# A two-layer transformer kernel: the first layer's feed-forward goes over to seven block products, with its hidden values passed through DRAM

## The chip, the core and the metric

The kernel runs on one core of one Trainium2 chip. The metric is the device time of one execution in microseconds; the time of before is the median of three runs. The profile is of one more execution of the same program.

## The reference, cut to what matters

Two layers work on 1024 latent tokens and 256 context tokens of width 1024 (the context leaves after layer 0). Each layer is a mixer (attention with a second branch) and a feed-forward (SwiGLU, hidden width 2816), each followed by a residual sum and a layer norm. Six vectors per layer, the modulation, are computed from `c` and `c_ctx`.

```python
def swiglu(h, w_in, w_out):
    a, g = jnp.split(h @ w_in, 2, axis=-1)
    return (jax.nn.silu(g) * a) @ w_out

        x = layer_norm(ALPHA * x + g1 * y, ln1_g[l], ln1_b[l])
        x = layer_norm(ALPHA * x + g2 * swiglu(x * (1.0 + sc2) + sh2, ffn_w_in[l], ffn_w_out[l]), ln2_g[l], ln2_b[l])
        if with_ctx_out:
            xc = layer_norm(ALPHA * xc + cg1 * yc, ln1_g[l], ln1_b[l])
            xc = layer_norm(ALPHA * xc + cg2 * swiglu(xc * (1.0 + csc2) + csh2, ffn_w_in[l], ffn_w_out[l]),
                            ln2_g[l], ln2_b[l])
```

## The kernel before, in words

All is fp32. A matrix product is made of three fp32r matmuls: each operand is split into a high part (a cast, mostly on ScalarE) and a low part (a subtraction, on GpSimd or VectorE), and high x high, high x low and low x high are summed in PSUM (`mm3`, L234; `split`, L222). Activations stay transposed: `X[c][b]` holds channel chunk c (8 of 128 channels) of token block b, split. Blocks 0 and 1 are 512 latents each, block 2 is the 256 context tokens. A weight unit is 128 x 1024 floats: `wunit` (L227) loads it into one of two `raw` buffers, and splits it into one of three `w` buffers of the same ring.

All loads and stores are issued by SyncE (SP), in order. A scheduler that simulates the engines puts the instructions of each engine in order when the program is built; program order is the priority, and `high_priority` shifts it. The hardware keeps that order on each engine. The exception is layer 1's attention, whose order is written out by hand.

**Output projection, then feed-forward of layer 0.** `out_proj` (L974) goes over the blocks 0, 1, 2: eight output chunks of matmuls, added into `ACC` (the residual, L362), then `ln_block` (L364): transposes, statistics, normalisation in place, transposes back, and for each chunk the modulated value split into X and the residual for the next sum back into ACC. The norm of one block runs beside the matmuls of the next; that of block 2 has `early` (L559) beside it, the matmuls of hidden chunk 0 for token block 0.

`ffn` (L573) goes over the 22 hidden chunks in pairs. `hidden` (L589) makes, per chunk and block, 24 matmuls for the a half and 24 for the gate half, then `gate` (L548): silu on ScalarE, product on VectorE, split by VectorE and GpSimd into a `hid` buffer. The output weights of the pair follow, and `outs` (L607): for each block and each of eight output chunks six matmuls, then one addition into ACC on VectorE (L362). The last pair's `outs` alternate with the norm. Between these pieces `pump` takes one step at a time of the modulation of layer 1 (`ada_vec`, L306): a 512 KB load, four or eight multiply-adds on VectorE (L323, L325), and after every second step column sums on TensorE (L330). 48 such steps lie in this stage.

**Feed-forward of layer 1.** `ffn_fast` (L763) has two passes. The first makes the hidden values: chunks 0 and 1 in the usual way (`plain`, L736), the others in pairs, with seven block products in place of eight. The 8 channel chunks and the two token blocks make a 2 x 2 block matrix of the activations, and the pair of hidden chunks with the two channel halves one of the weights. `x_sums` (L696) forms sums of the activation blocks in ACC, and `t_split` (L709) splits them into T. `weights` (L785) loads the two units, splits them into two `w` tiles, makes four sums in place and splits these into two `ws` tiles, of which there are three. `blocks` (L830) makes seven products of 12 matmuls each and combines them with additions on ScalarE and VectorE. The hidden values go to DRAM (`hs`). The residual was stored to `accs` by the norm (`full`, L409). The second pass loads hidden values back into the slots of X (`hid`, L902), splits them, and does the output matmuls as above; ACC is loaded again by `load_acc`. In the last pair of the first pass, both halves do products 1, 2 and 3 first (`begin`), as products 2 and 3 free the slots of X that the second pass fills first.

```python
            for j, x in ((2, b22), (3, b12), (4, b21)):
                self.t_split(j, c, x, 'gvg'[j - 2])
...
            pair(NHC - 2, (1, 2, 3))
```

Of the kernel before, what the change touches and what calls it, by code (L numbers as in the profile page):

```python
# [17 lines left out]
P = 128  # L18
# [16 lines left out]
NV = 5  # L35
# [4 lines left out]
EARLY = ((0, 0),), ((0, 0), (0, 1))  # L40
# [14 lines left out]
FAST, LASTB = (1,), 6  # L55
# [121 lines left out]
class K:  # L177
# [128 lines left out]
    def ada_vec(self, l, v, nvec, srcs, pspool, pstag, bufs=2, q0=0, abufs=None):  # L306
# [29 lines left out]
        for q in range(q0, 4):  # L336
            for kh in range(2):
                self.side.append(lambda q=q, kh=kh: piece(q, kh))


    def acc_open(self, l, blks, first=True):
        if l in FAST and first:
# [4 lines left out]
        self.ehp, self.eh = p, {}  # L347
        self.ACC = [p.tile([P, 8, BLKN[b]], F32, name=f"ACC{l}_{b}") for b in blks]
# [15 lines left out]
    def ln_block(self, b, pools, sc=None, sh=None, acc='keep', out=None, lnb=None, eng=None, tiles=None, group=1,  # L364
# [38 lines left out]
        for c in range(8):  # L403
# [5 lines left out]
            if full:  # L409
                self.affine('a', t, pb, self.lna[:, 0, c:c + 1], self.lna[:, 1, c:c + 1])  # L410
                self.dma(self.accs[c, :, BLK0[b]:BLK0[b] + n], t)
                t = A[:, c, :]
                self.affine('av'[b == 0 or c % 2], t, pb, sc[:, c:c + 1], sh[:, c:c + 1])
                self.split(t, x[:, 0, :], x[:, 1, :], 'a', 'g' if b == 0 else 'vg'[c % 2])
                continue
# [132 lines left out]
    def gate(self, wp, tag, pa, pg, h, n):  # L548

        nc = self.nc  # L550
        sg = self.tile(wp, [P, 512], F32, tag, bufs=1 if tag == "sgx" else 2)
        nc.scalar.activation(sg[:, :n], pg[:, :n], AF.Silu)
        nc.vector.tensor_tensor(out=sg[:, :n], in0=pa[:, :n], in1=sg[:, :n], op=ALU.mult)
        self.split(sg[:, :n], h[:, 0, :n], h[:, 1, :n], 'v', 'g')

    def hidden_w(self, l, hc):
        return [self.wunit(self.I[f'fi{l}'][j * NHC + hc], 'a', 'v' if hc < 2 else 'g') for j in range(2)]

    def early(self, l, pp, wp):  # L559

        for hc, b in EARLY[l]:
            if hc not in self.eh:
                self.eh[hc] = (self.hidden_w(l, hc), {})
            (wa, wg), hb = self.eh[hc]
            pa = self.tile(pp, [P, 512], F32, "op")
            self.fm_block(pa, wa, self.X, b)
            pg = self.tile(pp, [P, 512], F32, "op")
            self.fm_block(pg, wg, self.X, b)
            hb[b] = self.tile(self.ehp, [P, 2, BLKN[b]], F32R, f"eh{hc}_{b}")
            with self.tc.high_priority(HPE) if HPE else ExitStack():  # L570
                self.gate(wp, "sgx", pa, pg, hb[b], BLKN[b])

    def ffn(self, l, blks):  # L573
        nc, tc, I = self.nc, self.tc, self.I
        gv = lambda b: self.mod[:, l, 5, 1 if b == 2 else 0, :]

        with tc.tile_pool(name=f"ffn{l}", bufs=1, reuse_waits="tile") as fp:
            side, wst = ExitStack(), ExitStack()
            wx = None
            if l == 1:  # L580
                self.ctxstack.close()
                wx = wst.enter_context(tc.tile_pool(name="wx", bufs=1, side="right", reuse_waits="tile"))
            pp = side.enter_context(tc.tile_pool(name=f"ffps{l}", bufs=8, space=PSUM, reuse_waits="tile"))
            if l == 0:
                self.adp = side.enter_context(tc.tile_pool(name="ffad", bufs=1, reuse_waits="tile"))
                for v in range(6):
                    self.ada_vec(1, v, 2 if v < 2 else 1, [I['ad1'][v * 8 + j] for j in range(8)], pp, "f", abufs=1)

            def hidden(hc):  # L589

                (wa, wg), hs = self.eh.pop(hc) if hc in self.eh else (self.hidden_w(l, hc), {})
                rest = [b for b in blks if b not in hs]
                h = self.tile(fp, [P, 2, NTOK], F32R, "hid", bufs=3)
                pas = []
                for b in rest:
                    pa = self.tile(pp, [P, 512], F32, "f")
                    self.fm_block(pa[:, :BLKN[b]], wa, self.X, b)
                    pas.append(pa)
                for b, pa in zip(rest, pas):
                    pg = self.tile(pp, [P, 512], F32, "f")  # L600
                    self.fm_block(pg[:, :BLKN[b]], wg, self.X, b)
                    hs[b] = h[:, :, BLK0[b]:BLK0[b] + BLKN[b]]
                    self.gate(fp, "sg", pa, pg, hs[b], BLKN[b])
                    self.pump(1)
                return hs

            def outs(pp, tag, hs, us, b, o=0, n=None):  # L607
                n = n or BLKN[b]
                for f in range(8):
                    ps = self.tile(pp, [P, 512], F32, tag)  # L610
                    for i, u in enumerate(us):
                        w = u.rearrange("p s (f m) -> p s f m", m=P)
                        self.mm3(ps[:, :n], w[:, 0, f], w[:, 1, f], hs[i][b][:, 0, o:o + n], hs[i][b][:, 1, o:o + n],
                                 i == 0, i == len(us) - 1)
                    self.add_out(ps, f, b, gv(b), o, n)


            end = NHC - 2
            for h0 in range(0, end, 2):
                hcs = range(h0, min(h0 + 2, end))  # L620
                hs = [hidden(hc) for hc in hcs]
                us = [self.wunit(I[f'fo{l}'][hc], 'a', 'g') for hc in hcs]
                for b in blks:
                    outs(pp, "f", hs, us, b)
            last = range(end, NHC)
            ws, us, hs = {}, {}, {hc: {} for hc in last}
            if l == 0:
                hs = {hc: hidden(hc) for hc in last}
                us = {hc: self.wunit(I['fo0'][hc], 'a', 'v') for hc in last}
            self.pump(1000)  # L630
            side.close()
            with ExitStack() as es:
                pp, pools = self.tail_pools(es, f"ft{l}", *TP[l])
                self.ltb = LTB[2]
                if l == 0:
                    vec = self.ln_vecs(0, 2, 3, 2, 1, 0, 1, "02")
                else:
                    bc = self.tile(pools[0], [P, 2, D], F32, "lnbc")
                    self.dma(bc, I['lnbc'])

                    def final(r, nt):
                        bv = bc.rearrange("p k (c m) -> p k c m", m=P)
                        n = NV if r < NLAT - 2 * P else NVL
                        for k, op in ((0, ALU.mult), (1, ALU.add)):
                            self.tt('v', nt[:, :n], nt[:, :n], bv[:, k, :n], op)
                            self.tt('g', nt[:, n:], nt[:, n:], bv[:, k, n:], op)
                        o = self.O['out'][r:r + P, :].rearrange("t (c m) -> t c m", m=P)
                        for c in (slice(0, n), slice(n, 8)) if r >= NLAT - DSP * P else (slice(0, 8),):
                            self.dma(o[:, c], nt[:, c])
                ht = {hc: self.tile(fp, [P, 2, NTOK], F32R, "hid", bufs=3) for hc in last if l}  # L650

                def last_hidden(b, o, n):
                    for hc in last:
                        if hc not in ws:
                            ws[hc] = [self.wunit(I[f'fi{l}'][j * NHC + hc], 'a', 'g', wx if hc == end else None) for j in range(2)]
                        pq = []
                        for w in ws[hc]:
                            pq.append(self.tile(pp, [P, 512], F32, "op"))
                            self.fm_block(pq[-1][:, :n], w, self.X, b, o, n)
                        t = BLK0[b] + o  # L660
                        hs[hc][b] = ht[hc][:, :, BLK0[b]:BLK0[b] + BLKN[b]]
                        self.gate(fp, "sg", *pq, ht[hc][:, :, t:t + n], n)
                    for hc in last:
# [8 lines left out]
                for k, (b, o, n) in enumerate(segs):  # L672
                    if l == 1:
                        for seg in segs[k and k + SEGA:k + SEGA + 1]:
                            last_hidden(*seg)
# [946 lines left out]
```

## Time and profile before

| | us |
|---|---|
| median of 3 runs (3249.15 to 3252.54) | 3250.75 |
| the profiled execution's own time | 3247.87 |
| its span, first to last instruction | 3246.1 |
| output projection of layer 0, about | 710 to 865 |
| feed-forward of layer 0, to the last hidden chunk | 865 to 1751 |
| first pass of layer 1's feed-forward, about | 2555 to 2983 |
| second pass, to the end | 2989 to 3246 |

The rows of a profile name the line of the kernel, the engine, the operation and out <- in by the tiles' names, with shapes, the count, busy time and mean duration. Busy times of matmuls overlap, since they are pipelined. Idle time before an instruction is put down to what ended it. Tables of windows give the busy time of each engine in a stretch, the granted clock of TensorE (1.00 is 2.4 GHz, 0.50 is 1.2 GHz), the busy share of the DMA engines and the bytes moved.

### The profile page before, as it was taken

To read this page: it belongs to the slowest core of one execution; us is meant where nothing else is said; L and a number is where in the kernel's file an instruction comes from. 1 tells how busy PE (TensorE), PEld (TensorE's weight loads), DVE (VectorE), ACT (ScalarE), POOL (GpSimd) and SP (SyncE) were. 2 spreads that over 40 slices of the span, in tenths; PEclk is the share of its full clock that TensorE was granted. 3 is DMA by queue.
4 is the path that set the end of the run, shared out by engine and by line. 5 is a ranking of instruction groups with operands and counts; after the bars stand their busy time and mean duration, and the time that the engine had idled before them with its cause. 6 is when DMAs were issued, how large, how long until landed. Compare 5 with 4: busy or idle time off the path is not lost. (4 is left out here: it accounts for less than half of the span.)

```text
span 3246.1 us, 47796 instructions
## 1 busy us (share of the span) xinstructions
PE 3140.1 (97%) x18580; PEld 2770.4 (85%) x18580; DVE 1952.3 (60%) x3385; ACT 1096.8 (34%) x1930; POOL 1421.9 (44%) x1292
## 2 busy tenths in 40 slices
PE   8899999999999999999999999999999899999998
PEld 8888999988888888888888898988888788887877
DVE  6998777766755444444224597368874544445655
ACT  2235676652311011111111434367763422222221
POOL 3665777771322222222221244247763444443344
PEclk8899999999999999999999999999999999999999
DMA  5354122132222222221111234323213122225332
GB/s 218 111 192 126 30 49 53 29 110 85 74 72 72 75 73 77 73 79 65 40 36 38 91 122 129 109 67 93 80 48 130 53 84 78 84 85 169 104 111 59
DMA packets 157010, 282.07 MB, mean 87 GB/s; under 512 B 27120, under 2 KB 97520, under 8 KB 156656
## 3 DMA queue, kind: packets, MB, share of 16 engines
q1 hardware_dynamic: 156784, 279.01, 26.9%
q8 instruction: 147, 2.41, 0.3%
q14 instruction: 79, 0.65, 0.1%
HBM read 223.64 MB, written 55.31 MB: 86 GB/s over the span
## 5 line engine op out<-in xcount | busy, mean ns | idle before, releaser
L214 POOL TENSOR_TENSOR w<-raw,w 128x1024 fp32r<-128x1024 f32 x120 | 266.4, 2225 | 629.5 <-ACT w L206 533.9
L236 PE MATMUL f<-X,w 128*128 128x512 f32 (+1 forms) x1336 | 488.3, 365 | 16.8 <-ACT w L206 7.4
L237 PE MATMUL f<-X,w 128*128 128x512 f32 (+1 forms) x1336 | 485.0, 363 | 1.6 <-POOL X L214 1.6
L238 PE MATMUL f<-X,w 128*128 128x512 f32 (+1 forms) x1336 | 479.3, 362 | 0.0
L206 ACT CAST w<-raw 128x1024 fp32r<-128x1024 f32 (+1 forms) x170 | 168.2, 998 | 796.5 <-issue 395.1
L362 DVE SCALAR_TENSOR_TENSOR ACC<-f,mod,ACC 128x512 f32<-128x512 f32 (+1 forms) x368 | 244.6, 689 | 128.0 <-PE f L238 127.5
L236 PEld LDWEIGHTS f<-X,w 128*128 128x128 f32 x1336 | 253.7, 190 | 56.9 <-DVE ACC L362 8.2
L526 PE MATMUL acc<-w,X 128*128 128x256 f32 x1008 | 293.6, 292 | 8.3 <-ACT u L1096 4.9
L325 DVE SCALAR_TENSOR_TENSOR ada<-adraw,silu_c,ada 128x256 f32<-128x256 f32 x490 | 291.2, 631 | 5.9 <-DMA adraw<-in_ad 2.9
L528 PE MATMUL acc<-w,X 128*128 128x256 f32 x1008 | 292.9, 291 | 0.0
L527 PE MATMUL acc<-w,X 128*128 128x256 f32 x1008 | 292.6, 290 | 0.0
L237 PEld LDWEIGHTS f<-X,w 128*128 128x128 f32 x1336 | 253.7, 190 | 40.4 <-POOL X L214 2.1
L238 PEld LDWEIGHTS f<-X,w 128*128 128x128 f32 x1336 | 253.1, 189 | 39.9 <-POOL w L214 0.4
L214 POOL TENSOR_TENSOR pp<-e,pp 128x512 fp32r<-128x512 f32 x156 | 203.4, 1310 | 36.2 <-ACT pp L206 30.4
L526 PEld LDWEIGHTS acc<-w,X 128*128 128x128 f32 x1008 | 199.0, 198 | 9.2 <-ACT u L1096 5.1
L527 PEld LDWEIGHTS acc<-w,X 128*128 128x128 f32 x1008 | 199.0, 197 | 0.0
L528 PEld LDWEIGHTS acc<-w,X 128*128 128x128 f32 x1008 | 199.0, 198 | 0.0
L1252 ACT ACTIVATE e<-ss 128x512 f32<-128x512 f32 x252 | 145.3, 596 | 86.1 <-PE ss L1250 79.0
L214 POOL TENSOR_TENSOR hid<-sg,hid 128x512 fp32r<-128x512 f32 (+1 forms) x65 | 77.1, 1187 | 213.2 <-DVE hid L208 201.9
L237 PE MATMUL f<-hid,w 128*128 128x512 f32 (+1 forms) x472 | 166.8, 353 | 0.0
L236 PE MATMUL f<-hid,w 128*128 128x512 f32 (+1 forms) x472 | 166.7, 353 | 0.0
L238 PE MATMUL f<-hid,w 128*128 128x512 f32 (+1 forms) x472 | 166.7, 353 | 0.0
(344 smaller groups left out, 8103.5 us busy)
## 6 DMA issues: line engine op xcount, KB each, us to landing
raw<-in_fi SPq DMA_DIRECT2D x88, 512.0 KB, 3.6
adraw<-in_ad SPq DMA_DIRECT2D x86, 512.0 KB, 3.6
raw<-in_fo SPq DMA_DIRECT2D x44, 512.0 KB, 3.5
qs<-stg SPq DMA_DIRECT2D x27, 512.0 KB, 3.9
qd<-qs SPq DMA_DIRECT2D x192, 64.0 KB, 2.3
q<-qs SPq DMA_DIRECT2D x180, 64.0 KB, 2.3
raw<-hs SPq DMA_DIRECT2D x22, 512.0 KB, 3.5
ks<-stg SPq DMA_DIRECT2D x20, 512.0 KB, 2.8
```

The lines of the kernel that those rows point to most:

```text
L206: nc.scalar.copy(out=out, in_=in_)
L214: eng.tensor_tensor(out=out, in0=a, in1=b, op=op)
L236: mm(ps, lhsT=wh, rhs=xh, start=start, stop=False)
L237: mm(ps, lhsT=wh, rhs=xl, start=False, stop=False)
L238: mm(ps, lhsT=wl, rhs=xh, start=False, stop=stop)
L325: nc.vector.scalar_tensor_tensor(out=a, in0=rv[:, k], scalar=s, in1=a, op0=ALU.mult, op1=ALU.add)
L362: self.nc.vector.scalar_tensor_tensor(out=a, in0=ps[:, :n], scalar=g[:, f:f + 1], in1=a, op0=ALU.mult, op1=ALU.add)
L526: mm(o, lhsT=xh, rhs=w[:, 0, k], start=st, stop=False)
L527: mm(o, lhsT=xh, rhs=w[:, 1, k], start=False, stop=False)
L528: mm(o, lhsT=xl, rhs=w[:, 0, k], start=False, stop=sp)
L1252: nc.scalar.activation(e, S, AF.Exp)
```

## The change

Layer 0 calls `ffn_fast` as well, and `ffn`, `hidden`, `gate`, `early` are gone. What it does:

- `out_proj` calls `early_fast` and `x_sums` for both layers; for layer 0 `early_fast` issues no matmuls, and `x_sums` makes the sums without splitting them. The norm is `full` for both layers: it stores the residual to a new DRAM tensor `accr` and leaves the modulated value in ACC. The context's ACC is a pool of its own, closed after the projection.
- Layer 0 makes chunks 0 and 1 plainly for all three blocks, then splits T, then goes over the ten pairs with seven products for the latents; the context's 256 tokens are multiplied plainly with the two `w` tiles (`ctx`).
- `weights` makes its four tiles at once, with `ws` in two buffers, and the products use them in another order (`lhs`). For both layers the last half-pair does products 1, 2, 3 (and the context) first; `begin` is gone, so the gate half of the last pair keeps the usual order. In layer 1 the a half of chunk 1 is split into a `ws` tile.
- Layer 1's modulation is pumped in both passes: vectors 0 to 2 in the first, 3 to 5 in the second, one piece after each block.
- `load_acc(0)` is issued with a priority shift of 400 in both layers.

```diff
-EARLY = ((0, 0),), ((0, 0), (0, 1))
-FAST, LASTB = (1,), 6
+LASTB, HPA = (2, 6), 400
...
+    def x_sums(self, split):
+        a, b = self.ACC[:2]
+        for c in range(4):
+            b11, b12, b21, b22 = a[:, c, :], b[:, c, :], a[:, c + 4, :], b[:, c + 4, :]
+            self.tt('v', b11, b12, b11, ALU.subtract)
+            self.tt('v', b12, b22, b12, ALU.subtract)
+            self.tt('v', b22, b22, b11, ALU.subtract)
+            self.tt('v', b21, b21, b22, ALU.subtract)
+            if split:
+                for j in (2, 3, 4):
+                    self.t_split(j, c, 'gvg'[j - 2])
...
+    def early_fast(self, l, pp):
+        self.hs = self.dram.tile([NHC, P, NTOK], F32, name=f"hs{l}")
+        self.wu, self.sg = {}, {}
+        for j, i in () if l == 0 else ((1, 0), (0, 0), (1, 1)):
+            self.plain(l, pp, "op", (j, i, 0))
+
+    def ffn_fast(self, l, blks):
...
+        if l == 0:
+            self.t_open(0)
+            for i in range(2):
+                for b in ((0, 1, 2), (1, 0, 2))[i]:
+                    for j in (1, 0):
+                        self.plain(l, pp, "f", (j, i, b))
+            for j in (2, 3, 4):
+                for c in range(4):
+                    self.t_split(j, c, 'vg'[c % 2])
+        else:
+            self.wsp = self.ws_open()
+            for x in (((1, 0, 1), (0, 0, 1), (1, 1, 1)), ((0, 1, 1),), ((0, 1, 0),)):
+                self.plain(l, pp, "f", *x)
...
+        lhs = {1: (0, 0), 2: (0, 1), 4: (1, 1), 5: (2, 0), 6: (2, 1), 7: (3, 0), 3: (3, 1)}
...
+                self.adp = fp
+                for v in range(6):
+                    self.ada_vec(1, v, 2 if v < 2 else 1, [I['ad1'][v * 8 + j] for j in range(8)], pp, "f", bufs=1,
+                                 qs=range(4) if v < 3 else range(0))
...
+            def weights(j, h0):
+                raws, ws = [], []
+                for i in range(2):
+                    raw = self.tile(self.ring, [P, 1024], F32, "raw", bufs=2)
+                    self.dma(raw, I[f'fi{l}'][j * NHC + h0 + i])
+                    raws.append(raw)
+                    w = self.tile(self.ring, [P, 2, 1024], F32R, "w", bufs=3)
+                    k = slice(512 * i if l else 0, 1024)
+                    self.split(raw[:, k], w[:, 0, k], w[:, 1, k], 'a', 'g')
+                    ws.append(w)
...
+                for raw in raws[::-1]:
+                    w = self.tile(wsp, [P, 2, 1024], F32R, "ws", bufs=2)
+                    self.split(raw, w[:, 0, :], w[:, 1, :], 'a', 'g')
+                    ws.append(w)
+                return ws
...
+                o = [otile() if i else ctile() for i in range(4)]
+                p1 = bank()
+                product(p1, 1, ws)
+                self.copy('a', o[0], p1)
+                if last:
+                    product(p1, 2, ws, True)
+                    p3 = bank()
+                    product(p3, 3, ws)
+                    ctx(0)
+                    ctx(1)
+                p6 = bank()
+                product(p6, 6, ws)
+                self.tt('v', o[1], p6, o[0], ALU.add)
+                if not last:
+                    product(p1, 2, ws, True)
+                done(0, p1, o[0])
+                if not last:
+                    ctx(0)
+                p7 = bank()
+                product(p7, 7, ws)
...
+                p5 = bank()
+                product(p5, 5, ws)
...
+                product(p7, 4, ws, True)
...
+                else:
+                    ctx(1)
+                    product(p5, 3, ws, True)
...
+                blocks(weights(1, h0), False, silu, silu_ctx)
+                self.pump(1)
+                blocks(weights(0, h0), h0 == NHC - 2, mult, mult_ctx)
+                self.pump(1 + h0 // 2 % 2)
+
+            for h0 in range(2, NHC, 2):
+                pair(h0)
...
+                if 2 in blks:
+                    raw, x = self.tile(fp, [P, NCTX], F32, "hrx", bufs=2), slot(hc)[2]
+                    self.dma(raw, hs[hc, :, NLAT:])
+                    self.split(raw, x[:, 0, :], x[:, 1, :], 'a', 'g')
...
+                self.adp = fp
+                for v in range(3, 6):
+                    self.ada_vec(1, v, 1, [I['ad1'][v * 8 + j] for j in range(8)], pp, "f", bufs=1)
             for h0 in range(0, end, 2):
                 us = [self.wunit(I[f'fo{l}'][hc], 'a', 'g') for hc in (h0, h0 + 1)]
                 if h0 == 0:
-                    load_acc(0)
+                    with tc.high_priority(HPA):
+                        load_acc(0)
                 h.update({hc: hid(hc) for hc in range(h0 + 2, min(h0 + 4, NHC))})
...
                 for b in blks:
                     outs(pp, "f", [h[h0], h[h0 + 1]], us, b)
+                    self.pump(1)
...
-        k.ffn(0, (0, 1, 2))
+        k.ffn_fast(0, (0, 1, 2))
```

## Rows read from the trace of the kernel before

**Rows 1.** The page's part 1: engine, busy us, share of the span, instructions.
```profile
PE 3140.1 (97%) x18580; PEld 2770.4 (85%) x18580; DVE 1952.3 (60%) x3385; ACT 1096.8 (34%) x1930; POOL 1421.9 (44%) x1292
```
**Rows 2.** Windows: layer 0's feed-forward, and layer 1's first and second pass.
```profile
core 0: us, PE busy (x) PEld busy (x) DVE busy (x) ACT busy (x) POOL busy (x), PEclk, DMA share, GB/s
865.00:1752.00 887.00, 886.50 (x4690) 766.63 (x4691) 383.27 (x669) 101.69 (x138) 226.05 (x133) 1.00 0.21 67
2600.00:2900.00 300.00, 300.00 (x1326) 248.49 (x1325) 133.84 (x176) 86.41 (x112) 138.67 (x65) 1.00 0.26 84
```
**Rows 3.** TensorE in order of time: start, duration; two neighbours of each width.
```profile
1747.09 0.39 PE L238 MATMUL f<-X,w 128*128 128x512 f32 x1
1747.32 0.39 PE L236 MATMUL f<-X,w 128*128 128x512 f32 x1
...
1748.91 0.28 PE L238 MATMUL f<-X,w 128*128 128x256 f32 x1
1749.03 0.28 PE L236 MATMUL f<-X,w 128*128 128x256 f32 x1
```
**Rows 4.** TensorE's groups by form, 865 to 1752 us.
```profile
L236 PE MATMUL f<-X,w 128*128 128x512 f32 x688 | 270.3, 393 | 1.4 <-ACT ACC L218 1.4
...
L236 PE MATMUL f<-X,w 128*128 128x256 f32 x352 | 100.1, 284 | 0.0
...
L330 PE MATMUL f<-ones,ada 128*128 128x1 f32 x128 | 15.7, 233 | 0.0
```
**Rows 5.** TensorE in order of time, around the last norm of layer 0's projection.
```profile
847.42 0.48 PE L236 MATMUL op<-X,w 128*128 128x512 f32 x1
...
856.37 1.03 PE L379 MATMUL lnt<-c_ident,ACC 128*128 128x128 f32 x8
...
859.51 0.39 PE L238 MATMUL op<-X,w 128*128 128x512 f32 x1
...
865.50 0.50 PE L236 MATMUL f<-X,w 128*128 128x512 f32 x1 [1.37 <-ACT ACC L218]
```
**Rows 6.** GpSimd in order of time: its last split of token block 1.
```profile
854.50 1.29 POOL L214 TENSOR_TENSOR X<-lt,X 128x512 fp32r<-128x512 f32 x1 [0.43 <-DVE X L208]
```
**Rows 7.** Windows of 5 us after two idle stretches of layer 1.
```profile
2575.00:2580.00 5.00, 2.08 (x5) 1.70 (x6) 1.48 (x2) 3.49 (x5) 5.00 (x4) 0.50 0.14 52
...
2990.00:2995.00 5.00, 5.00 (x15) 3.86 (x15) 4.89 (x8) 0.00 (x0) 0.00 (x0) 0.60 1.05 393
```
**Rows 8.** VectorE in order of time: two activation sums of layer 1.
```profile
2561.27 0.68 DVE L214 TENSOR_TENSOR ACC<-ACC 128x512 f32<-128x512 f32 x1
...
2562.47 1.77 DVE L214 TENSOR_TENSOR ACC<-ACC,ACC 128x512 f32<-128x512 f32 x1
```
**Rows 9.** Groups of GpSimd, ScalarE and VectorE in layer 1's first pass, 2600 to 2900 us.
```profile
L214 POOL TENSOR_TENSOR ws<-raw,ws 128x1024 fp32r<-128x1024 f32 x32 | 79.7, 2512 | 48.8 <-ACT ws L206 48.8
...
L206 ACT CAST ws<-raw 128x1024 fp32r<-128x1024 f32 x32 | 32.6, 1050 | 41.6 <-DVE raw L214 39.0 <-PE f L731 2.6
...
L214 DVE TENSOR_TENSOR raw<-raw,raw 128x512 f32<-128x512 f32 x48 | 34.1, 711 | 58.9 <-POOL w L214 58.5
```
**Rows 10.** The page's part 6: KB each, median us from issue to landing.
```profile
raw<-hs SPq DMA_DIRECT2D x22, 512.0 KB, 3.5
```
**Rows 11.** TensorE's waits, 2540 to 3000 us: total, times, longest.
```profile
PE f L236 <- ACT w L206: 7.4, 1, 7.4
PE f L236 <- DVE ACC L362: 5.9, 1, 5.9
```
**Rows 12.** VectorE's groups by form, 900 to 1700 us; the last row 3000 to 3170 us.
```profile
L325 DVE SCALAR_TENSOR_TENSOR ada<-adraw,silu_c,ada 128x256 f32<-128x256 f32 x196 | 129.4, 677 | 2.7
L362 DVE SCALAR_TENSOR_TENSOR ACC<-f,mod,ACC 128x512 f32<-128x512 f32 x160 | 117.4, 747 | 61.9 <-PE f L238 61.8
L362 DVE SCALAR_TENSOR_TENSOR ACC<-f,mod,ACC 128x256 f32<-128x256 f32 x80 | 38.7, 484 | 16.5 <-PE f L238 16.5
...
L214 DVE TENSOR_TENSOR X<-raw,X 128x512 fp32r<-128x512 f32 x17 | 20.0, 1179 | 12.4 <-ACT X L206 12.4
```

More of the change, by code (lines that the diff above doesn't have):

```diff
@@ L335, in piece @@
                     op0=ALU.add, op1=ALU.add)
-        for q in range(q0, 4):
+        for q in range(q0, 4) if qs is None else qs:
             for kh in range(2):
@@ L341, in acc_open @@
     def acc_open(self, l, blks, first=True):
-        if l in FAST and first:
+        if l == 1 and first:
             self.ebst = ExitStack()
@@ L346, in acc_open @@
         p = self.accst.enter_context(self.tc.tile_pool(name=f"acc{l}", bufs=1, reuse_waits="tile"))
-        self.ehp, self.eh = p, {}
-        self.ACC = [p.tile([P, 8, BLKN[b]], F32, name=f"ACC{l}_{b}") for b in blks]
+        self.ACC = [p.tile([P, 8, BLKN[b]], F32, name=f"ACC{l}_{b}") for b in blks if b < 2 or not first]
+        if first and 2 in blks:
+            self.acc2st = ExitStack()
+            p = self.acc2st.enter_context(self.tc.tile_pool(name="accx", bufs=1, reuse_waits="tile"))
+            self.ACC.append(p.tile([P, 8, BLKN[2]], F32, name="ACCx"))
     def acc_load(self, l, c, b):
@@ L544, in tm_group @@
         return ws
[L548 to L571, printed above, removed]
@@ L696, in x_sums @@
-    def x_sums(self):
-        a, b = self.ACC
+    def x_sums(self, split):
+        a, b = self.ACC[:2]
         for c in range(4):
@@ L741, in plain @@
             if (j, i) not in self.wu:
-                self.wu[j, i] = self.wunit(self.I[f'fi{l}'][j * NHC + i], 'a', 'g')
-            pss.append(self.tile(pp, [P, 512], F32, tag, bufs=8 if tag == "f" else None))
+                where = (self.wsp, "ws", 2) if l == 1 and (j, i) == (0, 1) else ()
+                self.wu[j, i] = self.wunit(self.I[f'fi{l}'][j * NHC + i], 'a', 'g', *where)
+            pss.append(self.tile(pp, [P, 512], F32, tag)[:, :BLKN[b]])
         for k in range(8):
@@ L916, in outs @@
                 for f in range(8):
[L917 removed]
+                    ps = self.tile(pp, [P, 512], F32, tag)
                     for i, u in enumerate(us):
@@ L1014, in out_proj @@
                     wst.close()
-                    if l in FAST:
-                        self.t_open(l)
-                self.ln_block(b, pools, v[:, 0], v[:, 1], lnb=LNB[l], eng=LNE[l], full=l in FAST)
-            if l in FAST:
-                self.early_fast(l, pp)
-                self.x_sums()
-            else:
-                self.early(l, pp, wp)
+                    if l == 1:
+                        self.t_open(1)
+                self.ln_block(b, pools, v[:, 0], v[:, 1], lnb=LNB[l], eng=LNE[l], full=True)
+            self.early_fast(l, pp)
+            self.x_sums(l == 1)
             self.pump(1000)
+        if l == 0:
+            self.acc2st.close()
     def in0(self):
```

268 lines of the change are left out of this document (72 added, 196 removed).

## The prediction

> **What bounds the kernel now.** I read the page's busy times first, then a table of windows, the groups by form, the order of time and the waits of TensorE. TensorE is busy for 97% of the span, VectorE for 60%, the others less [rows 1]. In the windows of layer 0's feed-forward (865 to 1752 us) TensorE is busy for 886.5 of 887.0 us at full clock, while VectorE, ScalarE and GpSimd are busy 43%, 11% and 25% and the DMA engines 21% [rows 2]. So this stage is worth what TensorE does in it, and nothing that the other engines are spared counts. A busy TensorE is not one at its peak, so I take the price of a matmul from the distance of two starts: 0.227 us for 512 columns, 0.120 us for 256 [rows 3]. This rebuilds the stage: 688 x 3 = 2064 input matmuls of 512 and 352 x 3 = 1056 of 256 [rows 4]; from the code (20 chunks, 8 output blocks, 3 matmuls) 960 output matmuls of 512 and 480 of 256; 3024 x 0.2267 + 1536 x 0.120 = 870 us. First start 865.50 [rows 5] and last window edge 1752 leave 16 us, the 128 column sums of L330 [rows 4]. There is no stall to win back here; only fewer matmuls shorten it.
>
> **The change, part by part.** The sum is made against the profiled execution, 3247.87 us (its span 3246.1 and 1.8 around it); the median of the three runs is 2.9 us above it, and I apply the sum to the median.
>
> **1. Fewer matmuls: -54.4 us.** For two hidden chunks the latents cost 2 chunks x 2 halves x 2 token blocks x 8 k x 3 = 192 matmuls of 512 columns; seven products cost 2 halves x 7 x 4 k x 3 = 168. 24 fewer, ten pairs (chunks 2 to 21): 240 x 0.2267 = 54.4. Context and output matmuls stay in number. Layer 1 runs its products in this form already: 1326 matmuls in 300 us, 0.226 us each, TensorE busy throughout [rows 2]. So the price holds for products.
>
> **2. Start of layer 0's feed-forward: +7.7 us.** Before, the 48 matmuls of `early` (chunk 0, block 0; 10.9 us) run from 847.42 to 859.7 under the layer norm of the context block, and the next input matmul starts at 865.50 [rows 5]. Now `early_fast` does nothing for layer 0. Its matmuls come after this norm, which can begin its statistics at 847.4 instead of 856.4. From there the norm took 9.1 us, so the first product could start at 856.5 at best; at worst at 865.5, since the norm now also stores its affine result through two `lt` tiles and ScalarE does that affine. I take 860, between them and nearer to the best, as block 1's norm still holds GpSimd until 855.8 [rows 6]. Having 10.9 us less done but starting 5.5 us earlier costs 5.4. TensorE then idles most of 847 to 860; after a shorter idle stretch in layer 1 it was granted 0.50 of the clock, 1.2 GHz, for a window of 5 us [rows 7], about 2.3 us lost. Bounds +1.9 and +13.2.
> The 16 `x_sums` on VectorE: 0.68 us each undisturbed, 1.77 us beside a busy GpSimd [rows 8], so 11 to 28 us; the twelve `t_split`s come after. Their cover is the 53 us of plain products of chunks 0 and 1; eight PSUM banks hold six blocks before a late VectorE stops TensorE. Nothing; without that cover, up to 17 us.
>
> **3. Weights of the first pass, 3 + 2 buffers: 0.** For each half of a pair (20 in layer 0, 20 in layer 1) ScalarE and GpSimd make four weight tiles and VectorE four sums, in a chain. Split 1.05 us on ScalarE, 2.5 on GpSimd, a sum 0.71 [rows 9]. With two `ws` buffers the third tile waits for product 5 of the block before, 13.6 us into layer 1's 19.0 us, and is first read by product 6 at 21.7: 13.6 + 1.05 + 2.5 = 17.2, 4.5 us early. The fourth waits for the end at 19.0, is ready at 22.6 and read at 27.2. In layer 0 the context blocks add 5.8 us to each block. Lower bound 0; the upper one is the first rival.
>
> **4. Traffic and queues: 0.** New are 24 stores of the residual in the norm, 66 stores and 44 loads of hidden values, and 24 loads of that residual. In layer 1 the same kind of load lands in 3.5 us [rows 10]. The second pass moves per pair two weight units, two hidden chunks and three modulation units, 3.9 MB in 27.5 us, 143 GB/s, against 393 GB/s seen at an entry of a pass [rows 7]. SP issues in order: a load whose `raw` is not free holds the loads behind it, but each is asked for a pair ahead. Bounds 0 and +4.
>
> **5. Entry of layer 0's second pass: +2.** Chunks 0 and 1 must be back, split, in the slots that products 2 and 3 free, and block 0 of the residual loaded. In the last half-pair 16.7 us of matmuls follow (48 x 0.2267 and 48 x 0.120), against some 7 us of splits; first products cover another 10.9 us until eight banks are full. Layer 1 shows the price of missing it: 5.9 us waiting on the first ACC addition and part of a window at 0.60 [rows 7, 11], 8 us. Bounds 0 and +8.
>
> **6. VectorE in the second pass: +3.** Per pair: 16 additions of 0.747, 8 of 0.484, two splits of 1.18 and three modulation pieces of 4 x 0.677 [rows 12]: 11.9 + 3.9 + 2.4 + 8.1 = 26.3 us, beside 96 x 0.2267 + 48 x 0.120 = 27.5 us of TensorE. Before, the same pieces lay in a stage in which VectorE was busy 43%. 24 pieces are gone after eight pairs. It fits, at 96%, and in-order waits will not always fit. Bounds 0 and +16 (2 us a pair). Here a rule speaks against the change. The rows first: the modulation operation takes 0.677 us on average while GpSimd splits, and a two-input sum 1.77 instead of 0.68 [rows 8, 12]. The Trainium skill, SBUF — State Buffer, "SBUF: two separate sides", says that VectorE with two SBUF inputs and GpSimd share a port pair that one holds for its whole instruction while the other stops. By it a piece of the second pass could lose a whole GpSimd split, 2.5 us, and the term would be near its upper bound; the trace agrees with the mechanism, and no row of before shows its size in such a pass.
>
> **7. Layer 1, entry of its second pass: -5.** The 5.9 us wait and the clock behind it [rows 7, 11] come from residual loads issued behind hidden and weight loads; now they have priority and land where `e` and `c` are free before the pass ends. Against this, the last pair's products 2 and 3 come only 10.9 us before its end (before, both halves did them first, some 20 us). Bounds -8 and +3.
>
> **8. Layer 1, first products: -4.** TensorE waits 7.4 us for a weight split [rows 11] that had to wait for one of three `w` tiles and then stood behind the T splits. Now this unit goes to `ws`, free from the start. Next late is the chain of splits on GpSimd, nearly full there, so I take half. Bounds -9 and +1.
>
> Sum: -54.4 + 7.7 + 2 + 3 - 5 - 4 = -50.7; 3250.75 - 50.7 = **3200 us**.
>
> **The rivals.** That fewer products are not fewer matmuls is excluded by the count; all rivals are stalls.
> *Weights come late in every half-pair (slower).* If both `ws` tiles are made only after the end of the block before, product 6 waits for 1.05 + 2 x 2.5 - 2.7 = 3.4 us; over 40 half-pairs 136 us, 3336. It decides from 50.7 / 40 = 1.3 us per half-pair on. For: layer 1 loses a `ws` buffer. Against: the 4.5 us of slack worked out above. 0.05.
> *VectorE bounds the second pass.* At 29 us a pair, 1.6 us lost eight times, term 6 becomes +13 and beyond: 3210 to 3215. This is the port rule's case. 0.12.
> *Entries at their dear ends, layer 1's waits stay.* -54.4 + 13.2 + 8 + 3 = -30: 3220. For: such stalls moved, not vanished, in layer 1. 0.13.
> *Entries at their cheap ends.* -54.4 + 1.9 - 8 - 9 = -69.5: 3181. 0.10.
> *Forecast*, 3192 to 3210: 0.60.
>
> **How the numbers follow.** A measurement tells about 0.2%, 6.5 us, from no change. Every case but the first rival lies below 3244, so faster 0.95; of that rival's 0.05, 0.04 is slower and 0.01 within the bound. The range 3184 to 3222 takes in the forecast, the VectorE case and most of the dear case; left out are the slower rival, most of the cheap case and a tail of the dear one, 0.16.
>
> **What would show it.** Input matmuls fewer by 240 with distances of 0.227 us; TensorE without waits through layer 0's first pass (else term 3); the first product of layer 0 near 860 us with a slow window behind it; waits on ACC additions inside layer 0's second pass (term 6) or only at its entry (term 5); the 7.4 and 5.9 us rows of layer 1 shorter. Repeated waits of product 6 on a `ws` split would make the forecast wrong.

## The result, and the profile after

The changed kernel takes **3304.51 us** (median of four runs, 3302.41 to 3308.65) against 3251.47 of the kernel before beside it: ratio **1.0166, interval 1.0148 to 1.0183**. It is 1.7% slower; 3200 was forecast, 3184 to 3222 the range. The profiled execution took 3302.55 us, span 3300.8, 54.7 longer than before's 3246.1.

The page's part 1 of the changed kernel, to set beside [rows 1], and the chain that ended last (its second line):

```profile
PE 3112.4 (94%) x18340; PEld 2737.2 (83%) x18340; DVE 2139.1 (65%) x3529; ACT 1198.6 (36%) x2092; POOL 1509.7 (46%) x1314
...
DMA raw<-in_fi 4%; PE S L1350 3%; PE o L1410 3%; DVE raw L213 2%; POOL ws L213 2%; PE op L237 1%; PE f L235 1%; PE f L236 1%; PE op L236 1%; PE op L235 1%; PE f L237 1%; POOL w L213 1%; PE pt L1071 1%; DVE o L213 1%; PE f L589 1%
```

The 240 matmuls are gone (18580 to 18340), as counted. But TensorE fell from 97% to 94% of a longer span, and loads, sums and splits of first-pass weights (`raw<-in_fi` 4%, `raw` and `ws` 2% each) now stand in the chain that ended last; in the chain of before all loads together have 1%. Windows of the changed kernel: layer 0's first pass, its second, and the stretch of layer 1's first pass that [rows 2] showed at 300.00 of 300:

```profile
core 0: us, PE busy (x) PEld busy (x) DVE busy (x) ACT busy (x) POOL busy (x), PEclk, DMA share, GB/s
865.00:1437.00 572.00, 566.29 (x3018) 488.42 (x3017) 304.59 (x440) 151.84 (x213) 220.76 (x97) 1.00 0.28 91
1437.00:1760.00 323.00, 281.49 (x1405) 241.03 (x1404) 235.58 (x362) 46.73 (x77) 88.47 (x63) 0.93 0.39 129
2600.00:2900.00 300.00, 276.39 (x1185) 223.69 (x1185) 130.44 (x159) 80.48 (x109) 125.91 (x61) 0.98 0.24 74
```

Layer 0's first pass, for which I watched the weights, is nearly full. Idle are its second pass (41.5 of 323 us) and, at 141 matmuls fewer than [rows 2] in the same 300 us, layer 1's first pass, whose matmuls the change left alone. TensorE's waits over the span (total us, times, longest):

```profile
PE f L329 <- DVE ada L324: 38.3, 5, 10.5
...
PE f L589 <- ACT ws L205: 18.6, 10, 4.4
PE f L589 <- DVE o L213: 13.2, 8, 2.2
...
PE lnt L381 <- DVE ACC L219: 6.5, 1, 6.5
```

The first lies wholly in layer 0's second pass, the next two in layer 1's first, the last at layer 0's start. One milestone parts the account in two: TensorE's first matmul of layer 1's feed-forward, before and after:

```profile
2550.53 0.80 PE L236 MATMUL f<-X,w 128*128 128x512 f32 x1 [0.71 <-ACT ACC L218]
```
```profile
2576.01 0.50 PE L235 MATMUL f<-X,w 128*128 128x512 f32 x1 [0.72 <-ACT ACC L217]
```

So all that lies ahead of layer 1's feed-forward is 25.5 us longer, although 54.4 us of matmuls are gone from it, and that feed-forward adds 29.2.

**The start.** TensorE in order of time; its counterpart is [rows 5]:

```profile
848.52 0.33 PE L381 MATMUL lnt<-c_ident,ACCx 128*128 128x128 f32 x1 [0.85 <-DVE ACCx L364]
...
855.36 1.09 PE L381 MATMUL lnt<-c_ident,ACCx 128*128 128x128 f32 x4 [6.52 <-DVE ACC L219]
...
862.03 0.69 PE L408 MATMUL lnb<-c_ident,ACCx 128*128 128x128 f32 x2 [5.58 <-ACT ACCx L217]
...
867.89 0.50 PE L235 MATMUL f<-X,w 128*128 128x512 f32 x1 [0.94 <-ACT ACCx L217]
```

The first input matmul comes 2.4 us later than before, with 10.9 us of products not done yet: 13.3 us lost. The norm's transposes wait for the PSUM bank that VectorE's affine of block 1 reads, and VectorE had `x_sums` in front of it.

**A modulation piece of the second pass**, on VectorE, GpSimd, SyncE's queue and TensorE (SyncE's row merges two issues, the first at 1572.84):

```profile
1572.28 0.47 DVE L324 SCALAR_TENSOR_TENSOR ada<-adraw,silu_c,ada 128x256 f32<-128x256 f32 x1
...
1577.47 0.48 DVE L324 SCALAR_TENSOR_TENSOR ada<-adraw,silu_c,ada 128x256 f32<-128x256 f32 x1 [1.69 <-DMA adraw<-in_ad]
1577.87 0.48 DVE L364 SCALAR_TENSOR_TENSOR ACC<-f,mod,ACC 128x256 f32<-128x256 f32 x1
1578.27 2.17 DVE L324 SCALAR_TENSOR_TENSOR ada<-adraw,silu_c,ada 128x256 f32<-128x256 f32 x1
...
1581.62 2.16 DVE L324 SCALAR_TENSOR_TENSOR ada<-adraw,silu_c,ada 128x256 f32<-128x256 f32 x1
...
1577.59 2.57 POOL L213 TENSOR_TENSOR w<-raw,w 128x1024 fp32r<-128x1024 f32 x1 [5.78 <-ACT w L205]
...
1580.99 2.52 POOL L213 TENSOR_TENSOR w<-raw,w 128x1024 fp32r<-128x1024 f32 x1
...
1572.84 11.30 SPq L193 DMA_DIRECT2D adraw<-in_ad  x2
...
1583.84 1.02 PE L329 MATMUL f<-ones,ada 128*128 128x1 f32 x4 [7.10 <-DVE ada L324]
...
1584.00:1589.00 5.00, 5.00 (x14) 4.13 (x15) 2.90 (x9) 0.00 (x0) 0.37 (x1) 0.50 0.61 210
```

`adraw` has one buffer. The load is issued at 1572.84, when the last multiply-add of the piece before (1572.28 + 0.47) has read it; the data is there at 1577.47, and four multiply-adds follow, two of them 2.17 us instead of 0.48 beside GpSimd's splits. TensorE, in order, stands for 7.10 us before four column sums of 1 us, with matmuls queued behind them; the clock is then granted at 0.50, its 1.2 GHz level, from 1584 to 1589 us (the last row).

**A half-pair of layer 1's first pass**, on GpSimd, ScalarE, SyncE's queue, TensorE and VectorE:

```profile
2862.42 2.40 POOL L213 TENSOR_TENSOR ws<-raw,ws 128x1024 fp32r<-128x1024 f32 x1 [2.55 <-ACT ws L205]
2870.84 2.40 POOL L213 TENSOR_TENSOR w<-raw,w 128x1024 fp32r<-128x1024 f32 x1 [6.03 <-ACT w L205]
2873.19 2.40 POOL L213 TENSOR_TENSOR ws<-raw,ws 128x1024 fp32r<-128x1024 f32 x1
...
2883.68 2.40 POOL L213 TENSOR_TENSOR ws<-raw,ws 128x1024 fp32r<-128x1024 f32 x1 [2.55 <-ACT ws L205]
...
2869.71 1.05 ACT L205 CAST w<-raw 128x1024 fp32r<-128x1024 f32 x1 [6.89 <-DMA raw<-in_fi]
2870.67 1.04 ACT L205 CAST ws<-raw 128x1024 fp32r<-128x1024 f32 x1
...
2882.55 1.04 ACT L205 CAST ws<-raw 128x1024 fp32r<-128x1024 f32 x1 [2.80 <-DVE raw L213]
...
2865.81 0.38 SPq L193 DMA_DIRECT2D raw<-in_fi  x1
...
2875.62 10.81 SPq L193 DMA_DIRECT2D raw<-in_fi  x2
...
2857.95 0.39 PE L589 MATMUL f<-X,w 128*128 128x512 f32 x1
...
2862.59 0.50 PE L589 MATMUL f<-T,w 128*128 128x512 f32 x1 [1.76 <-DVE o L213]
...
2865.67 0.39 PE L589 MATMUL f<-X,ws 128*128 128x512 f32 x1
...
2883.65 0.50 PE L589 MATMUL f<-T,ws 128*128 128x512 f32 x1 [1.73 <-ACT ws L205]
...
2860.51 1.42 DVE L213 TENSOR_TENSOR raw<-raw,raw 128x512 f32<-128x512 f32 x2
2861.85 1.48 DVE L213 TENSOR_TENSOR o<-f,o 128x512 f32<-128x512 f32 x2
```

The first `ws` split of one half-pair starts at 2862.42, that of the next at 2883.68: 21.3 us, where 84 matmuls take 19.0. Between them lies one closed round. The split ends and frees a `raw` (2864.8); the next half's first unit is loaded (2865.81, there at 2869.71) and cast; only behind that cast stands the cast of the half before's fourth tile (2870.67), GpSimd splits both in turn (to 2875.6); this frees the second `raw`, whose load (2875.62) lands at 2879.1; then come four sums, the cast, and the next `ws` split. Two loads, one after the other, in each round.

TensorE's order has a part in it. Product 1 of the next half (2857.95) runs ahead of products 4 (2862.59) and 3 (2865.67) of the half before. Product 3 is the last to read the fourth tile's `ws` buffer, which so comes free near 2868.6, some 10.6 us into the next half. TensorE's waits follow the late sums in two ways, mostly by turns: for the `ws` cast behind them (2883.65, product 6), or for an addition into `o` that VectorE takes behind them (2862.59, product 4; the sums end at 2861.93).

### The profile page after: what moved, and what is told of

Read it like the earlier page. It is cut to its first block, busy times and chain, and to the rows that moved or that the text cites. A ratio compares the mean times of both kernels' runs of the same rounds, so it can differ in the third digit from the quotient of the medians.

```text
span 3300.8 us, 48115 instructions
## 1 busy us (share of the span) xinstructions
PE 3112.4 (94%) x18340; PEld 2737.2 (83%) x18340; DVE 2139.1 (65%) x3529; ACT 1198.6 (36%) x2092; POOL 1509.7 (46%) x1314
## 5 line engine op out<-in xcount | busy, mean ns | idle before, releaser
L213 POOL TENSOR_TENSOR w<-raw,w 128x1024 fp32r<-128x1024 f32 (+1 forms) x125 | 284.5, 2278 | 587.8 <-ACT w L205 573.9
L235 PE MATMUL f<-X,w 128*128 128x512 f32 (+1 forms) x1176 | 411.2, 350 | 8.1 <-DVE ACC L364 6.4
L236 PE MATMUL f<-X,w 128*128 128x512 f32 (+1 forms) x1176 | 408.9, 348 | 1.5 <-POOL X L213 1.5
L237 PE MATMUL f<-X,w 128*128 128x512 f32 (+1 forms) x1176 | 395.7, 347 | 0.0
L324 DVE SCALAR_TENSOR_TENSOR ada<-adraw,silu_c,ada 128x256 f32<-128x256 f32 x490 | 316.6, 687 | 59.6 <-DMA adraw<-in_ad 57.9
L364 DVE SCALAR_TENSOR_TENSOR ACC<-f,mod,ACC 128x512 f32<-128x512 f32 (+1 forms) x368 | 236.1, 684 | 76.2 <-PE f L237 75.3
L213 POOL TENSOR_TENSOR ws<-raw,ws 128x1024 fp32r<-128x1024 f32 x81 | 196.9, 2431 | 141.1 <-ACT ws L205 137.6
L235 PEld LDWEIGHTS f<-X,w 128*128 128x128 f32 x1176 | 226.7, 193 | 39.1 <-DVE ACC L364 7.7
L236 PEld LDWEIGHTS f<-X,w 128*128 128x128 f32 x1176 | 226.5, 193 | 30.6 <-POOL X L213 1.9
L237 PEld LDWEIGHTS f<-X,w 128*128 128x128 f32 x1176 | 226.3, 192 | 28.9
L213 POOL TENSOR_TENSOR pp<-e,pp 128x512 fp32r<-128x512 f32 x156 | 203.8, 1313 | 35.0 <-ACT pp L205 29.2
L213 DVE TENSOR_TENSOR raw<-raw,raw 128x512 f32<-128x512 f32 x120 | 82.9, 690 | 153.4 <-DMA raw<-in_fi 144.7
L213 POOL TENSOR_TENSOR X<-raw,X 128x512 fp32r<-128x512 f32 x44 | 57.7, 1313 | 220.8 <-ACT X L205 220.8
L205 ACT CAST X<-raw 128x512 fp32r<-128x512 f32 x88 | 50.7, 619 | 286.3 <-DMA raw<-hs 281.8
```

Source lines behind the costliest of these rows:

```text
L205: nc.scalar.copy(out=out, in_=in_)
L213: eng.tensor_tensor(out=out, in0=a, in1=b, op=op)
L235: mm(ps, lhsT=wh, rhs=xh, start=start, stop=False)
L236: mm(ps, lhsT=wh, rhs=xl, start=False, stop=False)
L237: mm(ps, lhsT=wl, rhs=xh, start=False, stop=stop)
L324: nc.vector.scalar_tensor_tensor(out=a, in0=rv[:, k], scalar=s, in1=a, op0=ALU.mult, op1=ALU.add)
```

## The experiments

The kernel before ran beside each group of runs (medians 3249.6 to 3251.2); each figure is a median, with its ratio to before and the interval.

**Two raw buffers for the second pass's modulation.**

```diff
-                    self.ada_vec(1, v, 1, [...], pp, "f", bufs=1)
+                    self.ada_vec(1, v, 1, [...], pp, "f", bufs=2, abufs=1)
```

> Changed kernel with one edit: in layer 0's second pass the modulation's raw tile has two buffers instead of one (its accumulators keep one). Theory (one buffer): the load of a piece can be issued only after the last multiply-add of the piece before, so it lands too late for VectorE's order, and TensorE stands at the column sums, 38.3 us in five waits plus the slow clock behind each. Then the waits of the column sums in the second pass fall below 10 us and the time falls by 35 to 50 us, to 3255 to 3270. Rival (VectorE's work bounds the pass, port sharing with GpSimd's splits): the waits stay over 25 us and the time stays above 3290. Rival (queue order on SP holds the loads): waits stay, named on DMA adraw.

3268.29 us, 1.0057 [1.0038, 1.0075]: 36 less. TensorE's waits on `ada`, 1440 to 1780 us:

```profile
PE f L329 <- DVE ada L324: 8.1, 1, 8.1
```

The theory held: 38.3 us in five waits became one of 8.1, though VectorE has the same work beside the same splits. So the late load, and neither VectorE's throughput nor the shared port, made most of the loss; a smaller one from VectorE's order shows in the last run below.

**Layer 1's weights in 3 + 3 buffers.**

```diff
-                where = (self.wsp, "ws", 2) if l == 1 and (j, i) == (0, 1) else ()
+                where = ()
...
-            self.wsp = self.ws_open()
...
-        wsp = self.wsp if l == 1 else self.ws_open()
+        wsp = self.ws_open()
...
-                    w = self.tile(wsp, [P, 2, 1024], F32R, "ws", bufs=2)
+                    w = self.tile(wsp, [P, 2, 1024], F32R, "ws", bufs=2 + l)
```

> Changed kernel with layer 1's weights in 3 + 3 buffers again, opened where they were before the change (the unit of chunk 1 goes back to the ring); layer 0 untouched. Theory (the two buffers close a loop of latencies in layer 1's first pass, some 1.8 us in each of its 20 half-pairs): 35 us come back there and some 3 to 5 are lost at the first products, 3270 to 3276; the first pass of layer 1 has TensorE busy throughout. Rival (traffic of the hidden values or SP's order slows layer 1): the time stays above 3295, half-pairs of 20.8 us.

3272.31 us, 1.0067 [1.0052, 1.0082]: 32 less, as expected. The waits on `ws` and `o` in layer 1's first pass are gone; the 7.4 us wait of [rows 11] is back. A half-pair shows why, in GpSimd's and SyncE's rows (each merges two): the second `ws` split follows the first at once, and both loads leave within 2.7 us behind them (in the next half-pair within 2.8).

```profile
2856.50 4.76 POOL L213 TENSOR_TENSOR ws<-raw,ws 128x1024 fp32r<-128x1024 f32 x2 [1.89 <-ACT ws L205]
...
2858.93 2.70 SPq L193 DMA_DIRECT2D raw<-in_fi  x2
```

**Only the number of `ws` buffers.** The run before with `bufs=2` for `2 + l`.

> As the run with layer 1's weights in 3 + 3 buffers, with one number different: two ws buffers instead of three; the unit of chunk 1 stays in the ring, opened where it was before the change. Theory (the number of ws buffers alone makes the loop of latencies): the waits of 1 to 2 us per half-pair are back, TensorE waits over 25 us in layer 1's first pass, and the time is that of the changed kernel plus the 4 us of the first products, 3303 to 3310. Rival (the ws pool was late or crowded because the unit of chunk 1 lay in it): it stays at 3275.

3301.51 us, 1.0158 [1.0144, 1.0172]. From 1.0067 to 1.0158 is 0.91%, 29.6 us, for one buffer: the theory held. Waits in layer 1's feed-forward:

```profile
PE f L589 <- DVE o L213: 14.9, 9, 2.0
PE f L589 <- ACT ws L205: 13.7, 8, 1.9
```

**`x_sums` moved.** In the code they stand behind chunk 0's plain products.

```diff
-            self.x_sums(l == 1)
+            if l == 1:
+                self.x_sums(True)
...
                         self.plain(l, pp, "f", (j, i, b))
+                if i == 0:
+                    self.x_sums(False)
```

> Changed kernel with layer 0's 16 sums of x moved on VectorE behind the plain products of chunk 0, so that they no longer stand in front of the context norm's statistics. Theory (the sums delayed the norm): first product near 861 instead of 867.9, 5 to 8 us less, 3296 to 3300. Rival (the norm's own affine and its stores set the start): within 2 us of the changed kernel.

3305.84 us, 1.0167 [1.0152, 1.0182]: nothing. But the edit did not do what it says: VectorE's rows stand in the same order, sums in front of the statistics, with the first input matmul at 868.51. The order on an engine is laid out when the kernel is built, and sums whose inputs are there go ahead. The run tells nothing of either theory.

**The three edits together.**

> The three edits together. Theory (the three losses are separate and the 240 matmuls are worth 54 us): about 3304.5 - 40 - 32 - 6 = 3226, between 3212 and 3240, faster than the kernel before (3251). Rival (the products of layer 0 cost more than counted, or the losses move elsewhere): 3245 or more.

3237.49 us, 0.9962 [0.9952, 0.9973]: 67 less than the changed kernel, about 36 + 32 + 0, as the third edit did nothing. These two losses add.

**All modulation in the first pass.**

```diff
-                                 qs=range(4) if v < 3 else range(0))
+                                 qs=range(4))
...
-                self.pump(1)
+                self.pump(2 if l == 0 else 1)
                 blocks(weights(0, h0), h0 == NHC - 2, mult, mult_ctx)
-                self.pump(1 + h0 // 2 % 2)
+                self.pump(3)
...
-                    self.ada_vec(1, v, 1, [...], pp, "f", bufs=1)
```

> Changed kernel with all 48 modulation pieces in layer 0's first pass (2 and 3 pieces behind the halves of a pair) and none in its second pass; still one raw buffer. Theory (the second pass was lost to pieces that stand between the accumulations in VectorE's order): no wait on a column sum is left in the second pass and the time falls by as much as with two buffers (36 us) or some 10 more, to 3258 to 3270; the first pass, with VectorE at 53%, holds them without new waits of TensorE. Rival (the second pass is bound by its own loads and additions): it falls by less than 20 us. Rival (the first pass has no room): new waits on column sums there, 3280 or more.

3322.06 us, 1.0217 [1.0202, 1.0232]: 18 more than the changed kernel. Waits on `ada` in the first pass, and windows of both passes:

```profile
PE f L329 <- DVE ada L324: 54.3, 4, 16.1
```
```profile
865.00:1437.00 572.00, 512.92 (x2676) 441.11 (x2675) 320.32 (x494) 133.58 (x187) 193.40 (x84) 0.94 0.30 96
1437.00:1760.00 323.00, 319.54 (x1683) 275.55 (x1682) 199.07 (x298) 63.06 (x100) 108.26 (x74) 1.00 0.37 117
```

The theory was right about the second pass, which is whole (3.5 us idle), and wrong about the first: there the rival's new waits came. VectorE is busy for 56% of it, so its time in sum was not what lacked. Each of the four waits stands at the second of two column sums queued in a row (1155.72 and 1169.23 us for one pair): with one buffer the pieces come one load after the other. The accumulators have one buffer here too, so a multiply-add of the next piece waits for the sums of the last (1156.60); the run does not part the two.

**Early products for layer 0 again** (their gate's tile lies in the projection's pool).

```diff
...
-        for j, i in () if l == 0 else ((1, 0), (0, 0), (1, 1)):
+        for j, i in ((1, 0), (0, 0)) if l == 0 else ((1, 0), (0, 0), (1, 1)):
...
-                for b in ((0, 1, 2), (1, 0, 2))[i]:
+                for b in ((1, 2), (1, 0, 2))[i]:
```

> Changed kernel with the two plain products of chunk 0, block 0 of layer 0 run before the end of the context block's norm again, as they were before the change (48 matmuls, 10.9 us). Theory (the start lost 13 us because nothing filled the norm): 8 to 13 us less, 3291 to 3297, TensorE busy through 848 to 862. Rival (the start is set by VectorE's queue, sums ahead of the norm, and the work only moves): within 3 us of the changed kernel.

3299.81 us, 1.0148 [1.0133, 1.0163]: 5 less, between the two, with an interval that overlaps the changed kernel's. The matmuls fill the norm, but the next input matmul comes at 872.04 instead of 867.89: the norm itself is later.

**Early products, and the sums bound by a dependence.**

```diff
...
+            prev = self.lastv
             self.tt('v', b11, b12, b11, ALU.subtract)
+            if not split and c == 0:
+                self.tc.add_manual_dep(...)
```

> As the run before, and the 16 sums of x now held behind the context norm in VectorE's order. Theory (sums in front of the norm's statistics delayed it): the norm ends 4 to 6 us earlier than with the products alone, 3286 to 3292. Rival (the norm is then covered by the products, or set by its own chain over ScalarE and its two store buffers): same as the run before within 3 us.

3293.41 us (3287.23 to 3299.57), 1.0137 [1.012, 1.0154]: 11 less than the changed kernel, a little above what was expected. The dependence held only the first four sums behind the early products; the other twelve stayed free, but VectorE's order came out otherwise, with the norm's statistics from 853.9 to 857.7 instead of 852.0 to 859.3. TensorE:

```profile
853.54 0.60 PE L383 MATMUL lnt<-c_ident,ACCx 128*128 128x128 f32 x4
...
865.26 0.80 PE L237 MATMUL f<-X,w 128*128 128x512 f32 x1 [1.66 <-ACT ACCx L219]
```

The first input matmul is where it was before (865.50) with the 10.9 us done: 13 us of the start are back at this matmul. The next 14 start 0.43 us apart (granted clock 0.50 from 865 to 870 us), where the changed kernel's start 0.24 apart, so some 3 us go again. The medians give 11, and their intervals overlap with those of the run before: that the sums' place on VectorE was the cause is likely, not shown.

**Modulation in the first pass, 3 + 3 buffers and the start mended.**

> All together: modulation in the first pass, layer 1's weights in 3 + 3 buffers, early products and sums behind the norm. Theory (the 240 matmuls are worth 54 us once the three losses are mended): between 3200 and 3225, faster than the kernel before by 0.8 to 1.5%. Rival (the matmuls that went were partly cover for other work): above 3230.

3277.43 us, 1.008 [1.0065, 1.0095]: a miss, by the 53.3 us in four waits on `ada` that the first pass has here too.

**Two raw buffers, 3 + 3, the start mended.**

> Two raw buffers in the second pass of layer 0, layer 1's weights in 3 + 3, early products and sums behind the norm. Theory (the losses add): 3304.5 - 36 - 32 - 11 = 3225, between 3220 and 3231. Rival (start and second pass share a loss): 3235 or more.

3229.16 us, 0.9929 [0.9915, 0.9942]: within what the sum of the parts said.

**And no pieces in the second pass's first pair.**

```diff
-                    self.pump(1)
+                    self.pump(1 if h0 else 0)
```

> As the run before, and no modulation piece behind the three blocks of the first pair of layer 0's second pass. Theory (the 7.6 us wait that is left stands at the entry, where the piece's load is queued behind the residual's): that wait goes and with it part of a slow window, 8 to 12 us less, 3213 to 3218. Rival (the wait moves to the next pair, whose pieces then load as late): within 3 us of the run before.

3226.24 us, 0.9917 [0.9904, 0.9931]: nothing that can be told apart. The wait on `ada` at the entry, 9.5 us in the run before, went, but the waits on ACC additions rose from 9.6 to 15.8 us. The rival had the time right and not the mechanism: no wait on `ada` is left.

**Six pieces to the first pass, two a pair in the second.**

```diff
-                                 qs=range(4) if v < 3 else range(0))
+                                 qs=range(4 if v < 3 else 3 if v == 3 else 0))
...
-                self.pump(1 + h0 // 2 % 2)
+                self.pump(2)
...
-                    self.ada_vec(1, v, 1, [...], pp, "f", bufs=2, abufs=1)
+                    self.ada_vec(1, v, 1, [...], pp, "f", bufs=2, abufs=1, qs=range(3 if v == 3 else 0, 4))
...
-                    self.pump(1 if h0 else 0)
+                    self.pump(1 if h0 and b else 0)
```

> As the run before, with 6 of the 24 modulation pieces of layer 0's second pass moved into its first (30 there, at one piece behind the first half of a pair and two behind the second; one raw buffer), and the other 18 at two a pair, behind the second and third block. Theory (the 15.8 us of waits on ACC additions that are left are VectorE late by the pieces in its order): these waits fall below 8 us and the time by 5 to 10 us, 3216 to 3221. Rival (with one buffer the first pass has no room for two pieces in a row): a wait of over 5 us on a column sum in the first pass, and 3226 or more.

**3214.80 us, 0.9896 [0.9879, 0.9913]**: 11 less again (the two intervals just overlap), 1.0% faster than the kernel before and the best of all. The theory held: no wait on a column sum came in the first pass. Waits on ACC in the second pass, in the run before and in this one:

```profile
PE f L237 <- DVE ACC L366: 15.8, 11, 3.3
```
```profile
PE f L237 <- DVE ACC L366: 4.6, 3, 2.8
```

## Why the prediction was wrong

**Term 1 was right in count and price.** 240 matmuls went, and the changed kernel's 512-column matmuls of layer 0's feed-forward start 0.227 us apart (median), as before. The last run, with the stalls mended in part, is 35.5 us below before; no run shows the 54.4 whole.

**Term 3 failed, and it was the first rival.** "4.5 us early" followed the third tile from its own `ws` buffer, inside one half-pair. But its `raw` must first be loaded, and the second load waits for the fourth tile of the half before, whose cast stands behind the new half's first cast on ScalarE. And term 3 took the products in the order of the code, by which the fourth tile's buffer is free at the end of its half; on TensorE it came free some 10.6 us later, behind product 1 of the next half. The chain does not end with the half-pair; it closes on itself through two `raw` and two `ws` buffers, and a round takes 21.3 us where 19.0 are to be had. The rival's shape was right by half: of 17 waits of 1.1 to 2.2 us, one in most half-pairs, nine were for a `ws` tile (product 6 in the half-pair shown) and eight for VectorE's additions behind the late sums (product 4). Its size was not: layer 1 alone, 29.6 us for the buffer. Layer 0 runs the same chain without a wait on `ws`; its context blocks make each half-pair 5.8 us longer, which I take for the reason. I had given this 0.05, though the change took a buffer from a stage that had no idle time to show what the buffer was for.

**Terms 4 and 6 failed together.** Term 4 said that each load "is asked for a pair ahead"; with one `adraw` buffer none is. The diff says so, in `bufs=1` where two were the default, and the prediction did not read it. Term 6 then compared sums of busy time, 26.3 of 27.5 us, and put the price of order at +3, at most +16. The pass lost 41.5 us idle, 38.3 of them before column sums, and some slow clock; two buffers give 36 us back at unchanged work. What VectorE's order cost beyond that lies inside term 6's bounds: some 11 us, by the last run. The Trainium skill's rule that I weighed there (SBUF — State Buffer, "SBUF: two separate sides") is borne out by the rows: a multiply-add took 0.47 us while GpSimd was idle (1572.28) and 2.17 when a split was running (1578.27). From these rows the piece shown was some 3.4 us later, a part of its stand of 7.1 us. With the load ahead of need (two raw buffers), multiply-adds of 2.40 and 2.49 us stand in the trace too and cost little.

**Term 2 was right in kind and undersized:** +13.3, just past its dear end of +13.2. The first product came at 867.9, later than its worst case of 865.5, while the slow clock that it had priced at 2.3 us hardly showed (the first ten matmuls start 0.24 us apart). The cover that it named for `x_sums`, 53 us of plain products, does not hold, since VectorE took the sums in front of the norm's affine and statistics.

**Term 5 was undersized:** 3.2 us on the first ACC addition and 10.5 on the first piece, of which two buffers left 8.1, in place of +2 and past its bound of +8. **Term 7** held in this run, where the 5.9 us wait [rows 11] is 2.2, but in part by luck: with three `ws` buffers, and so without the late weights, the same wait is 4.6. **Term 8** about: the 7.4 us wait is gone, 5.6 us wait on the first `ws` tile instead (4.4 and 1.2), and first matmul to first product shrank from 42.6 to 39.3 us.

**The account of the spans:** -54.4 (counted) + 13.3 (start) + 66.6 between layer 0's first input matmul and layer 1's, as 25.5 remain, + 29.2 for layer 1 = 54.7. Of the 66.6, 63.1 lie ahead of the first output matmul of layer 0's last pair (1751.55 before, 1773.50 after). In that stretch TensorE is idle for 46.1 us, against 0.0 before. The other 17 are longer distances: the starts of neighbours exceed the median of their width by 18.0 us in sum, against 0.9 before, and 14.6 of this lie behind 1437 us, where the granted clock is 0.93. The last 3.5 us come behind 1773.50 and were not taken apart.

**What stays open:** the last run is 15 us above the forecast. Its trace has waits of 7.4 us at layer 1's first products and 4.6 at the entry of its second pass, as the run with 3 + 3 buffers alone has, so most of the 9 us that terms 7 and 8 had promised is missing in it; the rest was not taken apart. Nor was a third `raw` buffer tried in place of the third `ws`.

## What to carry to other kernels

When a change takes a buffer away, follow its tile round the whole loop, through every buffer that the chain reuses and every engine's order, until it meets itself; compare that period with the bound engine's, not the slack inside one round, and take the order of the products from the engine and not from the code. Busy time that fits says nothing of loads that can only be issued after the last use: a small in-order instruction behind such a load (here 1 us of column sums) stops the bound engine for most of the load and the work behind it (here 7.1 of 11.0 us). And after moving code, look at the engine's order in the trace before judging the idea.

## What the runs showed of the hardware

A stand of TensorE of 7.1 us cost more than itself: from 1584 to 1589 us, right behind it, the granted clock was 0.50 (1.2 GHz), and 512-column matmuls started 0.43 us apart or more. The modulation unit shown could be used 4.6 us after its issue; the median of all 86 in the changed kernel is 3.6 us to landing, near the 3.5 of a load of like size [rows 10]. So it was late mainly by when it was issued.

VectorE's multiply-add with both inputs in SBUF, due while a GpSimd split ran (1577.59 to 1580.16), ended 0.28 us behind it, at 1580.44.
